# Grouping a unit's attention steps on TensorE, and pinning the convolution norm to VectorE's order, in a hybrid encoder layer on one core

## The chip, the cores and the metric

The kernel runs on one core of one Trainium2 chip. The core has five engines with queues of their own that run in order: TensorE (PE, with its weight loads shown as PEld), VectorE (DVE), ScalarE (ACT), GpSimd (POOL), and SyncE (SP), which issues most DMAs. The metric is device time in microseconds for one execution, as the median of the runs. Less is better.

## The reference

One encoder layer over 2048 tokens of width 1024, all in float32:

```
q, k, v, u = split(rmsnorm(x) @ w_in)              # 8 heads of 64; rotary on q and k
att  = dilated attention: windows (128,1), (512,4), (2048,16), merged by a softmax of their log-denominators
conv = silu(layernorm(depthwise_conv31(a * sigmoid(g)) + b))        # 512 channels
h = x + concat(att, conv) @ w_out
h = h + cross attention(rmsnorm(h), rmsnorm(mem))    # 4 heads of 256, 256 memory rows
h = h + square(relu(rmsnorm(h) @ w_up)) @ w_down     # 4096 hidden
out = rmsnorm(h)
```

For each window and dilation a query block of 128 rows sees a band of keys: `s = q k^T / 8`, a mask, `p = exp(s - max)`, `o = p v / sum(p)`. The layernorm of the convolution needs the mean and the variance over 512 channels for every token.

## The kernel before

Matrix products are split into high and low parts (`mm3`, L198 to L202): three products of 128x512 columns for each 128x128 weight tile, so `L200`, `L201` and `L202` on TensorE are all the large products. Weights come by DMA into `raw`; ScalarE rounds them (`whi`, L190) and VectorE takes the rest (`wlo`, L191).

The work has stages. First the memory's products and the input projections: `lin` for q, k and the gated convolution input, and `v` (values), whose results ScalarE and VectorE evict into `vst` (L575, L576). Beside the last of these VectorE computes the convolution of the first 512 tokens: one multiply-add of 128x512 for each of 31 taps (`cacc`, L217). Then comes the far stage: attention of the first 512 tokens, in which the windows of dilation 16 are computed for all tokens, interleaved with the remaining gated input products. Then four post blocks of 512 tokens each: `o` (output projection), `xs` and `x` (cross attention), and eight times `up` and `dn` (the MLP). Beside post block p run, as sides, the near attention of the next 512 tokens (`att(p+1)`) and their convolution (`conv`). These three stretches are the passes. The last post block has no side.

An attention unit is one half of one head's work for one pattern: two query blocks. It has three steps, as a generator with two `yield`s between them:

1. the scores on TensorE (`s`, L1003, four products of 256 columns), then on VectorE the mask and the minimum (`att_probs`, L774), and on ScalarE the exponential (L775) into `sm`;
2. `att_turn`: four transposes of `sm` on TensorE (`pt`, L781), and the split of the result into half-precision `ph` (ScalarE, L784) and `pl` (VectorE, L785);
3. `att_pv`: twelve half-precision products of the probabilities with the values (`opt`, L789 to L791), and their eviction.

Far units (`att_far`, L857 and L858) do the same for four blocks. The loop `att` keeps three units in flight: u at step 1, a at step 2, b at step 3.

The convolution's norm, `conv_ln`, has its own steps: it loads the four channel blocks (`lc`), adds them (`lsum`, L240 to L242), sums columns on TensorE (`lps`), broadcasts the mean (`lrb`), squares, sums again, takes a reciprocal root with GpSimd's power (L177), broadcasts it (`lrc`, L185), and ends in Silu on ScalarE (L268), a split and two stores.

The order on each engine is not the order of the program alone. A planner in the framework places instructions by its own estimate of when they are ready. `weave` sets how often a side is advanced per step of the main work, and `after(stack, "pe")` ties what is issued under it on TensorE behind the last recorded TensorE instruction (`last["pe"]`); `"dve"` does the same on VectorE. `pinned(gen, names)` applies that to every step of a generator. Unpinned steps may be placed earlier on an engine than the work that the program issued before them. On SP the loads of keys and queries (`load_keys`) stand among those of the weights; GpSimd makes the second ordering of the queries (`turned`, L822).

The change touches `conv` (L705), the loop of `att` (L1079 to L1086) and the line that makes `ln0`, the norm of the first 512 tokens (L1138).

Of the kernel before, what the change touches and what calls it, by code (L numbers as in the profile page):

```python
# [43 lines left out]
def f(ap):  # L44
    return ap.bitcast(F32)


def hybrid_layer(ctx, tc, A, out):
# [3 lines left out]
    def pool(name, space=None, stack=ctx, side="left"):  # L52
        kw = {"reuse_waits": "tile", "side": side} if space is None else {"space": space}
        return stack.enter_context(tc.tile_pool(name=name, bufs=1, **kw))

    def dma(o, i, q=None):
        (q or nc.sync).dma_start(o, i)
# [10 lines left out]
    def ps(kind, name, shape=(P, 512), dtype=F32):  # L68

        if isinstance(banks[kind], str):  # L70
            kind = banks[kind]
        n = turn.get(kind, 0)
        turn[kind] = n + 1
        return psp.tile(list(shape), dtype, tag=f"bank{banks[kind][n % len(banks[kind])]}", name=name)
# [3 lines left out]
    def after(stack, *names):  # L78
        for nm in names:
            if nm in last:  # L80
                stack.enter_context(tc.issue_after(last[nm].ins))

    def pinned(gen, *names):

        while True:
            with ExitStack() as st:
                after(st, *names)
                if next(gen, st) is st:
                    return
            yield  # L90
# [11 lines left out]
    def drain(*gens):  # L102
        for g in gens:
            for _ in g:
                pass
# [57 lines left out]
    def gain(key, k):  # L163
        if key == "mem":
            return gm[:, k:k + 1]
        c = GV[key] + k
        return gv[:, c:c + 1]
# [8 lines left out]
    def newton_rsqrt(dst, v, t):  # L176
        POOL.tensor_tensor(dst, v, mhalf.to_broadcast([P, v.shape[1]]), op=ALU.pow)  # L177
        DVE.tensor_tensor(t, dst, dst, op=ALU.mult)
        DVE.scalar_tensor_tensor(t, t, -0.5, v, op0=ALU.mult, op1=ALU.mult)
        DVE.scalar_tensor_tensor(dst, t, 1.5, dst, op0=ALU.add, op1=ALU.mult)  # L180

    def bcast_rows(dst_ps, col, n):

        for j in range(n):
            PE.transpose(dst_ps[:, j * P:(j + 1) * P], col[:, j:j + 1].to_broadcast([P, P]), ident)  # L185
# [37 lines left out]
    def conv_ln(n, alloc):  # L223
        sl = slice(512 * n, 512 * (n + 1))
        cs = []
        for c in range(4):
            t = alloc(f"cs{c}", F32, f"lc{n}_{c}")
            dma(t, cscr[c][:, sl])
            cs.append(t)
        sm = alloc("sum", F32, f"lsum{n}")  # L230
        q = alloc("q", F32, f"lq{n}")
        col = [alloc(f"col{i}", F32, f"lcol{n}{i}", (P, 4)) for i in range(3)]

        def colsum(key):
            pc = ps("c", f"lps{n}{key}")
            for j in range(4):
                last["pe"] = PE.matmul(pc[:, j:j + 1], sm[:, j * P:(j + 1) * P], ones[:, 0:1], start=True, stop=True)
            return pc[:, 0:4]

        DVE.tensor_tensor(sm, cs[0], cs[1], op=ALU.add)  # L240
        DVE.tensor_tensor(sm, sm, cs[2], op=ALU.add)
        DVE.tensor_tensor(sm, sm, cs[3], op=ALU.add)  # L242
        yield
        yield
        DVE.tensor_scalar(col[0], colsum("m"), -1.0 / DCONV, None, op0=ALU.mult)
        yield
        rb = ps("c", f"lrb{n}")
        bcast_rows(rb, col[0], 4)
        for c in range(4):
            DVE.tensor_tensor(cs[c], cs[c], rb, op=ALU.add)  # L250
        ACT.activation(sm, cs[0], AF.Square)
        for c in range(1, 4):
            ACT.activation(q, cs[c], AF.Square)
            DVE.tensor_tensor(sm, sm, q, op=ALU.add)
        yield
        yield
        yield
        DVE.tensor_scalar(col[1], colsum("v"), 1.0 / DCONV, EPS, op0=ALU.mult, op1=ALU.add)
        yield
        newton_rsqrt(col[0], col[1], col[2])  # L260
        yield
        rb2 = ps("c", f"lrc{n}")
        bcast_rows(rb2, col[0], 4)
        for c in range(4):
            DVE.tensor_tensor(cs[c], cs[c], rb2, op=ALU.mult)
        yield
        for c in range(4):
            ACT.activation(cs[c], cs[c], AF.Silu, bias=gain("ln_b", c), scale=gain("ln_g", c))  # L268
        for c in range(4):
            th_ = alloc("hi", F32R, f"lh{n}_{c}")  # L270
            tl_ = alloc("lo", F32R, f"ll{n}_{c}")
            ACT.copy(th_, cs[c])
            POOL.tensor_tensor(tl_, cs[c], f(th_), op=ALU.subtract)
            dma(f(cath[4 + c][:, sl]), f(th_))
            dma(f(catl[4 + c][:, sl]), f(tl_))
            yield
# [404 lines left out]
    def ln_tiles(pl):  # L681
        def alloc(role, dtype, name, shape=(P, 512)):
            if role[:3] == "col":
                return pl.tile(list(shape), F32, tag="cl_" + role, name=name)
            if role[:2] == "cs":
                return pl.tile(list(shape), F32, tag="u" if role[2] < "2" else "acc", name=name, bufs=2)
            return pl.tile(list(shape), dtype, tag="vr", name=name, bufs=2)
        return alloc

    def conv_units(pl, n, cs=(0, 1, 2, 3), ahead=True):  # L690
        def alloc(role, shape, name):
            return pl.tile(list(shape), F32, tag=role, name=name, bufs=2)

        u = conv_load(cs[0], n, alloc)
        yield
        yield
        for i, c in enumerate(cs):
            nxt = conv_load(cs[i + 1], n, alloc) if ahead and i + 1 < len(cs) else None
            yield from conv_unit(c, n, alloc, u)
            u = nxt or (conv_load(cs[i + 1], n, alloc) if i + 1 < len(cs) else None)  # L700

    def conv(pl, n):

        yield from pinned(conv_units(pl, n), "dve")
        yield from conv_ln(n, ln_tiles(pl))  # L705

    def both(*gens):
        for _ in zip(*gens):
# [84 lines left out]
    def low_parts(pl, n, bufs, tag):  # L793

        t = [pl.tile([P, n], F32R, tag=f"{tag}{i}", name=f"{tag}{i}") for i in range(bufs)]
        for x in t:
            POOL.memset(f(x[64:P]), 0.0)
        return t
# [268 lines left out]
    def att(p, far=None):  # L1067


        comb = iter(())  # L1070

        def then(pr, o0):
            nonlocal comb
            drain(comb)
            comb = combine(p, pr, o0)
            next(comb)

        a = b = None
        for u in chain(att_units(p, far, then), (None, None)):  # L1079
            if u:  # L1080
                next(u)
            yield
            if a:
                next(a)
            if b:
                next(b, None)  # L1086
            next(comb, None)
            yield
            a, b = u, a
        for _ in comb:  # L1090
            yield
# [13 lines left out]
    def ahead(m):  # L1105
        raw = wp.tile([P, 8, P], F32, tag="raw", name=f"raw_o0{m}", bufs=2)
        dma(raw, wcols(w_out, m * P))
        yield
        wout[m] = wsplit2(wp, raw, f"o0{m}")
        turn_w[0] += 1  # L1110
        yield
# [3 lines left out]
    with ExitStack() as st:  # L1115
        p2_ = pool("att_far", stack=st, side="right")
        p2_.tile([P, 16, 144], F32R, tag="k3", name="k3", bufs=2)
        qlow3 = low_parts(p2_, 1024, 2, "ql3")
        p2_.tile([P, 176], F32, name="farpad")
        rest = pinned(pipeline(*(u for c in range(4) for u in glu(c, (2, 3), True)), ahead(0), ahead(1)), "pe")  # L1120
        for _ in range(38):
            next(rest)

        c01 = []

        def ln_alloc(role, dtype, name, shape=(P, 512)):

            if role[:3] == "col":
                return top.tile(list(shape), F32, tag="cl_" + role, name=name)
            if role in ("cs0", "cs1"):  # L1130
                if not c01:
                    c01.append(aq.tile([P, 2, 512], F32, tag="ld", name="lc01"))
                return c01[0][:, int(role[2])]
            if role in ("cs2", "cs3", "sum"):
                return aq.tile(list(shape), F32, tag={"cs2": "cth", "cs3": "ctl", "sum": "cat"}[role], name=name)
            return t2(name, dtype)

        ln0 = pinned(conv_ln(0, ln_alloc), "pe")  # L1138
        first = pinned(att(0, p2_), "pe")
        weave(islice(first, 50), (ln0, 0.33), (rest, 0.75))  # L1140
        drain(ln0)
        weave(islice(first, 74), (rest, 0.75))
        drain(rest)
# [458 lines left out]
```

## Time and profile before

| | us |
|---|---|
| median of 3 runs | 2862.2 |
| lowest and highest | 2858.24, 2862.79 |
| the profiled execution | 2865.75 |
| its span, first to last instruction | 2864.0 |

The profile is of one execution. On its page, groups of instructions stand by line, engine, operation and tiles, with their count, busy time and mean duration. TensorE's matrix products are pipelined: the next starts before the last one's shown end, so the time from start to start is what a product costs. A bracket at the end of a timeline row gives the idle time of the engine before that row, and what ended it. The windows view gives, for a stretch, the busy time of each engine and the clock that TensorE was granted (1.00 is full).

### The profile page before, as it was taken

The numbers are of one execution on the slowest core, as the hardware profiler recorded it, in microseconds if no ns is written. First come the engines' busy times: TensorE is split into PE (matmuls) and PEld (weight loads), VectorE is DVE, ScalarE is ACT, GpSimd is POOL, SyncE is SP. The second block draws the span as 40 slices with busy tenths as digits, with TensorE's granted clock in tenths as the row PEclk, the third lists the DMA queues.
The fourth block names the chain that finished last, engine by engine and source line by source line (L and its number), as shares of the span: only waits on it lengthen the run. The fifth ranks groups of instructions, "written<-read, shape, count | busy, mean of one in ns | idle before, by whom it ended". The sixth has DMA issues, their size and how long they took to land.

```text
span 2864.0 us, 41201 instructions
## 1 busy us (share of the span) xinstructions
PE 2807.4 (98%) x15440; PEld 2359.9 (82%) x15440; DVE 1960.8 (68%) x3473; ACT 1206.4 (42%) x2055; POOL 467.7 (16%) x483
## 2 busy tenths in 40 slices
PE   8999999999999999999999999999999999999998
PEld 7878899888788888888888888888888888888887
DVE  5736535455789777566887865579886646569886
ACT  5633211365544333434543344344433434444443
POOL 1337431131202011200021112001120110000000
PEclk9999999999999999999999999999999999999999
DMA  8979854699734544545444535534544455223332
GB/s 251 302 174 230 197 146 126 170 244 241 221 108 128 143 127 130 160 146 175 120 132 126 148 113 165 177 122 123 143 121 136 141 158 177 89 82 102 90 117 67
DMA packets 590730, 434.27 MB, mean 152 GB/s; under 512 B 191582, under 2 KB 508434, under 8 KB 590017
## 3 DMA queue, kind: packets, MB, share of 16 engines
q1 hardware_dynamic: 549776, 407.68, 50.5%
q10 hardware_dynamic: 38528, 17.93, 2.5%
q0 software_dynamic: 2224, 6.01, 0.6%
q8 instruction: 122, 2.00, 0.3%
q14 instruction: 80, 0.65, 0.1%
HBM read 340.42 MB, written 91.11 MB: 151 GB/s over the span
## 4 chain that ended last, share of the span: by engine, by line
PE 83%; DVE 8%; DMA 5%; issue 1%; ACT 1%; POOL 1%; SPq 1%; DVEq 0%; POOLq 0%; ACTq 0%
PE dn L200 8%; PE dn L201 8%; PE dn L202 8%; PE up L200 7%; PE up L202 7%; PE up L201 7%; PE lin L200 4%; PE lin L202 4%; PE lin L201 4%; PE o L200 2%; PE o L202 2%; PE o L201 2%; DVE cacc L217 2%; PE xs L200 2%; PE xs L202 2%; PE xs L201 2%
## 5 line engine op out<-in xcount | busy, mean ns | idle before, releaser
L200 PE MATMUL up<-mh,whi_u 128*128 128x512 f32 x1024 | 403.5, 394 | 0.4 <-ACT mh L1219 0.4
L201 PE MATMUL up<-ml,whi_u 128*128 128x512 f32 x1024 | 399.6, 390 | 2.1 <-DVE ml L1220 2.1
L202 PE MATMUL up<-mh,wlo_u 128*128 128x512 f32 x1024 | 399.1, 390 | 0.0
L217 DVE SCALAR_TENSOR_TENSOR cacc<-cu,cw,cacc 128x512 f32<-128x512 f32 x480 | 386.1, 804 | 5.4
L200 PE MATMUL dn<-hhh,whi_d 128*128 128x512 f32 x768 | 299.1, 399 | 1.1 <-ACT hhh L1331 1.1
L201 PE MATMUL dn<-hhl,whi_d 128*128 128x512 f32 x768 | 298.7, 391 | 0.7 <-DVE hhl L1332 0.7
L202 PE MATMUL dn<-hhh,wlo_d 128*128 128x512 f32 x768 | 298.2, 391 | 0.0
L190 ACT CAST whi_u<-raw_u 128x1024 fp32r<-128x1024 f32 x128 | 134.5, 1051 | 263.2 <-PE dn L201 188.7
L190 ACT CAST whi_d<-raw_d 128x1024 fp32r<-128x1024 f32 x100 | 105.1, 1051 | 319.9 <-PE up L201 281.5
L201 PEld LDWEIGHTS up<-ml,whi_u 128*128 128x128 f32 x1024 | 192.5, 188 | 40.9 <-DVE ml L1220 3.4
L202 PEld LDWEIGHTS up<-mh,wlo_u 128*128 128x128 f32 x1024 | 192.3, 188 | 40.4
L200 PEld LDWEIGHTS up<-mh,whi_u 128*128 128x128 f32 x1024 | 192.4, 188 | 38.0 <-ACT mh L1219 0.6
L191 DVE TENSOR_TENSOR wlo_u<-raw_u,whi_u 128x1024 fp32r<-128x1024 f32 x128 | 161.3, 1261 | 43.4 <-ACT whi_u L190 43.1
L1345 DVE TENSOR_TENSOR h<-h,dn 128x512 f32<-128x512 f32 x192 | 128.6, 683 | 84.7 <-PE dn L202 83.9
L1329 DVE SCALAR_TENSOR_TENSOR rl<-up,ssumx 128x512 f32<-128x512 f32 x96 | 66.0, 690 | 171.0 <-PE up L202 170.3
L774 DVE CUSTOM_DVE_ANT_0 sm<-s,mask 128x256 f32<-128x256 f32 (+1 forms) x384 | 128.6, 375 | 69.0 <-PE s L1003 45.2
L202 PEld LDWEIGHTS dn<-hhh,wlo_d 128*128 128x128 f32 x768 | 144.2, 188 | 30.7
L200 PEld LDWEIGHTS dn<-hhh,whi_d 128*128 128x128 f32 x768 | 143.7, 188 | 29.7 <-ACT hhh L1331 1.3
L201 PEld LDWEIGHTS dn<-hhl,whi_d 128*128 128x128 f32 x768 | 144.6, 188 | 28.3 <-DVE hhl L1332 1.5
L177 POOL TENSOR_TENSOR nr<-st_v,mhalf 128x4 f32<-128x4 f32 (+1 forms) x15 | 14.3, 951 | 817.2 <-DVE st_v L173 817.2
L775 ACT ACTIVATE sm<-sm,o 128x256 f32<-128x256 f32 (+1 forms) x288 | 116.5, 454 | 55.7 <-DVE o L774 55.3
L191 DVE TENSOR_TENSOR wlo_d<-raw_d,whi_d 128x1024 fp32r<-128x1024 f32 x100 | 128.2, 1282 | 14.2 <-ACT whi_d L190 14.1
(459 smaller groups left out, 7075.3 us busy)
## 6 DMA issues: line engine op xcount, KB each, us to landing
raw_u<-in_w_up_dram SPq DMA_DIRECT2D x128, 512.0 KB
raw_d<-in_w_down_dram SPq DMA_DIRECT2D x100, 512.0 KB
raw_o<-in_w_out_dram SPq DMA_DIRECT2D x32, 512.0 KB
raw_a<-ascr SPq DMA_DIRECT2D x32, 512.0 KB
raw_b<-bscr SPq DMA_DIRECT2D x32, 512.0 KB
b<-in_w_down_dram SPq DMA_DIRECT2D x28, 512.0 KB
k<-kscr SPq DMA_DIRECT2D x24, 512.0 KB
k<-kscr SPq DMA_DIRECT2D x8, 1152.0 KB
```

Source lines behind the costliest of these rows:

```text
L177: POOL.tensor_tensor(dst, v, mhalf.to_broadcast([P, v.shape[1]]), op=ALU.pow)
L190: ACT.copy(hi, raw)
L191: (lo_eng or DVE).tensor_tensor(lo, raw, f(hi), op=ALU.subtract)
L200: PE.matmul(o, lh, rh, start=first, stop=False, skip_group_check=more)
L201: PE.matmul(o, lh, rl, start=False, stop=False, skip_group_check=more)
L202: last["pe"] = PE.matmul(o, ll, rh, start=False, stop=end, skip_group_check=more)
L217: DVE.scalar_tensor_tensor(acc, u[:, t:t + 512], cw[:, c, t:t + 1], acc, op0=ALU.mult, op1=ALU.add)
L774: last["dve"] = DVE.tensor_tensor_reduce(dst, so, mask[:, 256 * m:256 * m + nk], 1.0, 3e38, ALU.add, ALU.min, mn)
L775: last["act"] = ACT.activation(dst, dst, AF.Exp, bias=mn, scale=-1.0)
L1329: last["dve"] = DVE.scalar_tensor_tensor(r, pt, 0.0, rsb, op0=ALU.max, op1=ALU.mult)
L1345: last["dve"] = DVE.tensor_tensor(hs[m], hs[m], pt, op=ALU.add)
```

## The change

In the passes the scores of unit u move from the beginning of the loop's turn to its end, after the transposes of unit a and the products of unit b, and the products and the scores are each tied behind the last recorded TensorE instruction. The far stage keeps the order that it had. The norm of the passes is pinned to VectorE's order, and the first norm, pinned to TensorE's before, to both.

```diff
     def conv(pl, n):
 
         yield from pinned(conv_units(pl, n), "dve")
-        yield from conv_ln(n, ln_tiles(pl))
+        yield from pinned(conv_ln(n, ln_tiles(pl)), "dve")
...
         for u in chain(att_units(p, far, then), (None, None)):
-            if u:
+            if u and far:
                 next(u)
             yield
-            if a:
-                next(a)
-            if b:
-                next(b, None)
+            for g in (a, b, None if far else u):
+                with ExitStack() as st:
+                    if not far and g is not a:
+                        after(st, "pe")
+                    if g:
+                        next(g, None)
             next(comb, None)
             yield
             a, b = u, a
...
-        ln0 = pinned(conv_ln(0, ln_alloc), "pe")
+        ln0 = pinned(conv_ln(0, ln_alloc), "pe", "dve")
```

## The prediction

> **What bounds the kernel now.** I read the page first, then the busy time by stage, then TensorE's own waits.
>
> ```profile
> span 2864.0 us, 41201 instructions
> PE 2807.4 (98%) x15440; PEld 2359.9 (82%) x15440; DVE 1960.8 (68%) x3473; ACT 1206.4 (42%) x2055; POOL 467.7 (16%) x483
> PE 83%; DVE 8%; DMA 5%; issue 1%; ACT 1%; POOL 1%; SPq 1%; DVEq 0%; POOLq 0%; ACTq 0%
> ```
>
> TensorE is busy for 98% of the span and carries 83% of the chain, so only what makes TensorE stand still or issue slower counts. Next, the windows: the far stage (541 to 770 us) and the three passes in which the near attention runs beside the post block (770 to 2262). The columns are length, TensorE busy, weight load, VectorE, ScalarE, GpSimd, granted clock, DMA.
>
> ```profile
> 541.00:770.00 229.00, 213.47 (x1847) 186.85 (x1847) 139.91 (x548) 137.12 (x326) 57.35 (x77) 0.96 0.87 229
> 770.00:1290.00 520.00, 518.09 (x2743) 428.27 (x2742) 391.86 (x653) 221.65 (x355) 74.00 (x75) 1.00 0.48 137
> 1290.00:1836.00 546.00, 543.70 (x2886) 450.26 (x2885) 397.15 (x670) 227.07 (x364) 76.13 (x76) 1.00 0.48 140
> 1836.00:2262.00 426.00, 423.78 (x2324) 351.05 (x2323) 327.96 (x566) 177.14 (x295) 55.06 (x56) 1.00 0.47 135
> ```
>
> The passes, where the grouping acts, hold 1492.00 - 1485.57 = 6.4 us of idle TensorE, at full clock: little can be won there by removing waits. The larger waits are earlier. From TensorE's list of waits over the span, and two of the same list for the passes alone:
>
> ```profile
> PE opt L791 <- DVE pl L785: 6.9, 9, 1.4
> PE s L858 <- DMA ql<-qfar: 4.3, 2, 2.2
> PE lin L200 <- DVE vst L576: 4.1, 1, 4.1
> ```
>
> ```profile
> PE up L201 <- DVE ml L1220: 2.1, 3, 0.9
> PE catT L948 <- POOL cat L940: 1.5, 2, 1.2
> ```
>
> The third row is one single wait. The timelines of VectorE and TensorE around it, and the windows behind it, say what it is:
>
> ```profile
> 506.08 0.69 DVE L240 TENSOR_TENSOR lsum<-lc 128x512 f32<-128x512 f32 x1 [9.44 <-DMA lc<-cscr]
> 521.58 0.69 DVE L242 TENSOR_TENSOR lsum<-lsum,lc 128x512 f32<-128x512 f32 x1 [5.97 <-DMA lc<-cscr]
> ```
>
> ```profile
> 513.56 0.80 PE L200 MATMUL lin<-xh,whi_g 128*128 128x512 f32 x1 [4.09 <-DVE vst L576]
> ```
>
> ```profile
> 513.50:518.30 4.80, 4.74 (x11) 3.78 (x12) 2.08 (x5) 0.00 (x0) 0.00 (x0) 0.50 0.35 111
> 518.30:524.00 5.70, 5.70 (x26) 4.70 (x26) 0.69 (x1) 0.60 (x1) 1.45 (x2) 1.00 0.99 255
> ```
>
> A sum of the convolution norm (L240) stands in VectorE's queue among the evictions of the value products and waits 9.44 us for a load. The evictions behind it (L576) come late, the banks stay full, and TensorE stops for 4.09 us. Then the clock is at half for 4.80 us.
>
> **The change part by part.**
>
> *The first norm (L1138, now pinned to VectorE too).* In the changed kernel's built order the three sums L240 to L242 no longer stand among the value evictions. They follow the score steps of the second far unit. The wait of 4.09 us goes. The half clock goes with it: 11 products took 4.80 us where the next window's 5.70 / 26 = 0.22 us each would give 2.4, so 2.4 are lost. Term 1 is -(4.1 + 2.4) = **-6.5**; its bounds are -6.5 and 0, zero if another wait of that length takes its place. Nothing of the norm is late next: the sums stand behind the last load's landing in these rows (521.58 us). The sums, 3 x 0.69 = 2.1 us, now lie in the far stage, where VectorE is busy 139.91 of 229.00 us; I cost them at nothing. If that cover fails, products there (`opt`, 6.9 us of waits already) wait up to 2.1 longer. The norm's later steps also move there by a few places, on ScalarE (Silu) and on SP, where half of one head's far queries are issued after two output stores; this end is bounded by the 2.2 us that such a load has cost once. I take 0 for both.
>
> *The norms of the passes (L705).* The same pin. No norm wait shows on TensorE's list for the passes, so it is worth 0; its limit is the 6.4 us of all waits there.
>
> *The grouping (L1079 to L1086).* No instruction is added or removed on TensorE (15,356 matrix instructions in both built orders). Three things change: the order inside a step, where the scores stand, and how long after them their transposes come.
>
> The first is a price for each time the stream goes from the half-precision products (`opt`) back to 32-bit work. A piece of the timeline in the first pass:
>
> ```profile
> 919.00 0.36 PE L1003 MATMUL s<-k,qt 128*128 128x256 f32 x1
> 919.20 0.29 PE L1003 MATMUL s<-k,ql 128*128 128x256 f32 x1
> 919.32 0.28 PE L1003 MATMUL s<-k,qt 128*128 128x256 f32 x1
> ...
> 920.55 0.48 PE L200 MATMUL up<-mh,whi_u 128*128 128x512 f32 x1
> 920.86 0.40 PE L201 MATMUL up<-ml,whi_u 128*128 128x512 f32 x1
> ```
>
> Starts tell the cost, since busy spans overlap. The scores at 919.00 follow `opt` products and hold the next start for 0.20 us, where the following one holds it 0.12; the `up` product at 920.55 follows `opt` and holds it 0.31 against the 0.22 above. So 0.08 to 0.09 us per change. Counted in the two built orders, `opt` is followed by something else 261 times before and 229 after (by matrix products 175 and 90, by scores 23 and 91, by transposes 37 and 41, by others 26 and 7). Term 2 is -32 x 0.08 = **-2.6**. Its bounds are -3 and 0.
>
> The second: scores were issued up to one step ahead of their unit's turn, and the planner could hoist them further. Now they stand behind the older unit's products. The buffers of keys and queries come free later, so SP issues those loads (two `qh`, one `ql`, one `k` per head) behind weight loads that they preceded, and GpSimd turns the queries (L822) later. Each is needed some three units on, about 30 us of TensorE work by the pitch above, so I cost it at 0; the limit is again 2.2 us per load that comes late.
>
> The third is the risk. By counting products between a unit's scores and its transposes, the median falls from about 18 us of TensorE work to about 9.5, and in 17 of 96 units to under 6.2. In that time VectorE must mask and take the minimum (L774) and ScalarE the exponential (L775). The quickest and one of the slowest in the first pass:
>
> ```profile
> 806.43 0.30 PE L1003 MATMUL s<-k,ql 128*128 128x256 f32 x1
> ```
>
> ```profile
> 806.76 0.42 DVE L774 CUSTOM_DVE_ANT_0 sm<-s,mask 128x256 f32<-128x256 f32 x1 [1.27 <-PE s L1003]
> ```
>
> ```profile
> 807.23 0.91 ACT L775 ACTIVATE sm<-sm,o 128x256 f32<-128x256 f32 x2
> ```
>
> ```profile
> 886.31 0.29 PE L1003 MATMUL s<-k,ql 128*128 128x256 f32 x1
> ```
>
> ```profile
> 892.82 0.90 ACT L775 ACTIVATE sm<-sm,low 128x256 f32<-128x256 f32 x2
> ```
>
> From the end of the scores to the end of the exponentials it takes 1.4 us where VectorE is free and 7.1 where it has a backlog. The tightest place is the start of the first pass's `up` stage, with some 2.2 us between the two. I walk it:
>
> ```profile
> 907.66 0.94 PE L1180 MATMUL nps<-ones,ssumx 128*128 128x1 f32 x8
> ```
>
> ```profile
> 911.25 0.16 DVE L173 TENSOR_SCALAR st_v<-nps 128x4 f32<-128x4 f32 x1
> ...
> 914.36 1.22 DVE L191 TENSOR_TENSOR wlo_d<-raw_d,whi_d 128x1024 fp32r<-128x1024 f32 x1
> 915.50 0.74 DVE L217 SCALAR_TENSOR_TENSOR cacc<-cu,cw,cacc 128x512 f32<-128x512 f32 x1
> 916.16 0.68 DVE L785 TENSOR_TENSOR pl<-pt,ph 128x512 f16<-128x512 f32 x1
> ```
>
> After the norm's column sums (`nps`) the new order has 31 `up` products (31 x 0.22 = 6.8 us), one attention group and four broadcasts (1.8) before the transposes: 8.6 us. VectorE has `st_v`, two weight splits (914.36 to 915.50, 1.14 each), four taps (0.66 each), one `pl` (0.6), two mask steps (0.7) and small steps (0.6), 6.8 in all, then ScalarE 0.9 and 0.1 for the hand-over: 7.8. If VectorE starts when `nps` ends there is no wait. If it is as late as in the rows (911.25 against 908.60, 2.65 us), the transposes wait 10.4 - 8.6 = 1.8. Eight more `up` products now precede `nps` (1.8 us), which eats most of that lateness, so I am nearer to 0 here. Over the 17 tight units I take four waits of about 1 us (the size of the 0.9 above), less 2 us of the present 6.4, which fall at the same `up` and `dn` starts. Term 3 is **+2**. Its bounds are -6.4 and +17 (each tight unit 1 us late).
>
> The sum is -6.5 - 2.6 + 2 = -7.1. The profiled execution took 2865.75 us (its span and 1.75 around it), 3.55 above the median of the runs, so 2858.65 for such an execution and 2862.2 - 7.1 = **2855.1** for the median.
>
> **The clock, row and rule.** What does a wait cost beyond itself?
>
> ```profile
> 736.68 0.20 PE L791 MATMUL opt<-v,pl 128*128 128x65 f16 x1 [1.39 <-DVE pl L785]
> ```
>
> ```profile
> 737.00:740.20 3.20, 3.20 (x14) 2.62 (x12) 0.22 (x1) 0.38 (x1) 1.43 (x2) 0.50 0.98 259
> 1760.00:1768.00 8.00, 6.82 (x33) 5.40 (x32) 5.76 (x6) 3.48 (x5) 3.25 (x2) 1.00 0.43 123
> ```
>
> A wait of 1.39 us was followed by 3.2 us at half clock, 1.6 us lost; the `catT` wait of 1.2 us, inside the second window, was not. So a new wait of 1.4 us or more is priced at itself plus 1.6. The Trainium skill (TensorE: Matmul & The Clock Gate, section "HAM oscillation — how this bites in real kernels") sets the rule at no idle gap above about 3.4 us, watched in a free-running window (Part 1). By that rule waits of this size are free of the clock, and the slower rival below would come to 2864.5 instead of 2869.3 (three times 1.6 less), no longer slower; the row at 736.68 disagrees with it, and I go by the row.
>
> **The rivals.**
> - *Slower: the transposes wait for VectorE.* Place: the `up` and `dn` starts of each pass. Price per pass: 1.8 + 1.6 for the clock at the walked place and 1.0 at two more, 5.4, or 16.2 in three passes; 2862.2 - 9.1 + 16.2 = 2869.3. It decides from 14.8 us in the passes, 4.9 per pass. For it: VectorE had backlogs of 7.1 us; against: the planner puts transposes where it holds them ready, and on TensorE's list for the passes stands no wait for an exponential.
> - *The stall moves.* The first norm's waits or the far queries' loads return the 6.5 us in the far stage: 2862.2 - 2.6 + 2 = 2861.6. For it: 15.5 us of idle there (229.00 - 213.47); against: the sums find VectorE free.
> - *Better: the present waits of the passes go too.* 2862.2 - 9.1 - 6.4 = 2846.7. Against: the two rows above show the post block's and the combine's waits, which the change doesn't touch.
> - *The grouping does not happen.* In the built order 48 of 96 groups stand whole, the others have matrix products inside. If the change of precision then costs what it did, 2862.2 - 6.5 = 2855.7.
>
> **How the numbers follow.** Forecast 0.52, slower 0.17, stall moves 0.15, better 0.10, no grouping 0.06. The bound between faster and same is 0.2%, 5.7 us, about what runs of this kernel can tell from no change. The forecast's own range is 2850 to 2859, so some 0.44 of its 0.52 is faster; with "better" and half of "no grouping" 0.57. Slower is most of its rival, 0.15. The rest, 0.28, is same. The range runs from 2847 to 2870, the two outer rivals.
>
> **What would show it.** Right: no `lin <- vst` wait and no half clock near 515 us; L240 after the first far scores; `opt` changes about 0.08 us each. Wrong: `pt <- sm` or `opt <- pl` rows with over 5 us per pass, half clock inside the passes, or far-stage idle above 20 us.

## The result, and the profile after

The change is slower: 2875.91 us (median; 2871.87 to 2882.25), against 2858.14 for the kernel before in the same comparison. The ratio is 1.0062, with a 95% interval of 1.0046 to 1.0077, or some 18 us. The forecast was 2855.1, below the kernel before; the time also lies outside its range. The profiled execution took 2882.25 us, the slowest of them, with a span of 2880.3. The lines of the changed kernel's page that answer to those shown of before (lines of the code behind the loop of `att`, which ended at L1086, have moved down by two):

```profile
span 2880.3 us, 41197 instructions
PE 2807.7 (97%) x15440; PEld 2362.3 (82%) x15440; DVE 1962.6 (68%) x3473; ACT 1213.0 (42%) x2055; POOL 463.7 (16%) x483
```

TensorE's busy time hardly moved (2807.4 before). The span grew by 16.3 us, so TensorE stands still longer. Its waits in the passes, as the list of waits has them (us in total, times, longest):

```profile
PE catT L948 <- POOL cat L940: 5.6, 2, 4.0
PE x L200 <- ACT xp L1261: 4.2, 3, 1.4
PE ptx L1272 <- DVE ptl L1275: 2.9, 3, 1.0
PE xs L200 <- ACT xp L1261: 2.4, 3, 0.8
PE x L200 <- ACT pth L1274: 2.0, 3, 0.7
PE up L200 <- DVE rl L1331: 1.9, 2, 0.9
PE pt L781 <- ACT ssumx L1312: 1.8, 1, 1.8
PE nrb L185 <- DVE nr L180: 1.4, 2, 0.7
PE dn L200 <- DVE h L1347: 0.4, 2, 0.2
```

These add up to 22.6 us, where the passes had 6.4. Rows 2 to 5 come three times each, once per pass, and all belong to the cross-attention's softmax: row 4 stands halfway through its scores (`xs`), where the banks come round again, row 2 at the hand-over from the scores to the output (`x`), rows 3 and 5 some 10 us into `x`. The first row is the combination of the attention parts. The walked place, `pt` at the start of `up`, waited once, for 1.8.

The windows of the changed kernel add the clock (columns as in the prediction: length, TensorE, weight load, VectorE, ScalarE, GpSimd, granted clock, DMA):

```profile
918.40:921.80 3.40, 3.40 (x20) 2.92 (x17) 3.40 (x6) 3.37 (x8) 0.00 (x0) 0.50 0.13 39
1218.70:1222.10 3.40, 3.40 (x11) 2.82 (x12) 2.30 (x3) 1.29 (x3) 0.00 (x0) 0.51 0.69 194
1409.90:1413.30 3.40, 3.40 (x23) 2.93 (x23) 1.10 (x2) 0.96 (x2) 0.00 (x0) 0.50 0.00 0
2027.70:2031.10 3.40, 3.40 (x10) 2.62 (x9) 3.40 (x5) 3.40 (x9) 1.68 (x4) 0.50 0.00 0
```

Four stretches at half clock, 1.7 us lost in each, 6.8 together; in the passes of before no window of 10 us was below 0.99. So the passes lost 16.2 us in waits (22.6 - 6.4) and 6.8 in clock in this execution.

What the change was to win by the first norm is there. The stretch of the old wait runs at full clock without idle time:

```profile
506.00:520.00 14.00, 14.00 (x79) 12.25 (x78) 0.85 (x2) 1.34 (x3) 1.84 (x2) 1.00 0.78 186
```

Up to the first `o` product the changed profile is 9.3 us ahead (it starts at 727.9 us, against 737.2). Not all of that is the first norm's: in the profiles of two kernels below that keep the old first norm (the hold on the norms of the passes alone, and the group alone) `o` starts at 729.7 and 729.4 us. From its first `o` to the first `o` of the last post block the change takes 26.3 us longer: TensorE's idle time in that stretch grows from 8.3 to 28.8 us, and it holds five stretches at half clock instead of one. The last post block is 0.7 shorter.

### The profile page after: what moved, and what is told of

The parts are those of the page before. It is cut to its first block, busy times and chain, and to the rows that moved or that the text cites. A ratio compares the mean times of both kernels' runs of the same rounds, so it can differ in the third digit from the quotient of the medians.

```text
span 2880.3 us, 41197 instructions
## 1 busy us (share of the span) xinstructions
PE 2807.7 (97%) x15440; PEld 2362.3 (82%) x15440; DVE 1962.6 (68%) x3473; ACT 1213.0 (42%) x2055; POOL 463.7 (16%) x483
## 5 line engine op out<-in xcount | busy, mean ns | idle before, releaser
L217 DVE SCALAR_TENSOR_TENSOR cacc<-cu,cw,cacc 128x512 f32<-128x512 f32 x480 | 392.5, 818 | 5.2
L822 POOL CAST qt<-qh 128x512 fp32r<-128x512 f32 x24 | 35.6, 1482 | 808.2 <-PE s L1003 802.6
```

The lines of the kernel that those rows point to most:

```text
L217: DVE.scalar_tensor_tensor(acc, u[:, t:t + 512], cw[:, c, t:t + 1], acc, op0=ALU.mult, op1=ALU.add)
L822: POOL.tensor_copy(d.rearrange("p (b i) -> p b i", b=4), t.rearrange("p (i b) -> p b i", b=4))
```

## The experiments

The theory formed from these two profiles: the group, not the norms, makes the loss, and makes it in the cross-attention, around the hand-over from `xs` to `x`, where each bank's softmax (a minimum and a scale on VectorE, an exponential on ScalarE) must end before the bank is used again. The rivals: the norm's hold does it; the group loses at many tight places; the group costs on its own and the norms give little back.

**The parts alone.** The first norm's hold alone:

```diff
-        ln0 = pinned(conv_ln(0, ln_alloc), "pe")
+        ln0 = pinned(conv_ln(0, ln_alloc), "pe", "dve")
```

> Only the first norm is pinned to VectorE's order; the grouping and the passes are as before. If the value stage's stall is the whole worth of this pin (theory A and theory B alike), TensorE's wait of 4.1 us for vst and the half clock after it are gone and the time is 6 to 9 us below before. If the stall only moves into the far stage, the time is within 2 us of before and the far stage's idle TensorE grows from 15.5 us to about 22.

Measured: 2851.88 us, ratio 0.9982 [0.9973, 0.9991], 5 us below the kernel before. The gain is real, somewhat under the expected size.

The hold on the norms of the passes alone:

```diff
-        yield from conv_ln(n, ln_tiles(pl))
+        yield from pinned(conv_ln(n, ln_tiles(pl)), "dve")
```

> Only the norms of the passes are pinned to VectorE's order. Theory A (the loss is the grouping's, in the cross attention): within 3 us of before. Theory B (the held-back norm delays the combine and the post block, as the longer waits for cat in the changed kernel suggest): 6 us or more above before, with waits of catT for cat of about 4 us.

Measured: 2858.20 us, 1.0008 [0.9998, 1.0018], no difference that can be told from none.

The group alone, the change with both norms put back:

```diff
-        yield from pinned(conv_ln(n, ln_tiles(pl)), "dve")
+        yield from conv_ln(n, ln_tiles(pl))
...
-        ln0 = pinned(conv_ln(0, ln_alloc), "pe", "dve")
+        ln0 = pinned(conv_ln(0, ln_alloc), "pe")
```

> Only the grouping; both norms as before. Theory A: 24 to 28 us above before, since the whole loss is here and the first norm's gain is missing. Theory B: 10 us above before or less. In both, the wait of 4.1 us for vst is back.

Measured: 2870.42 us, 1.0047 [1.0032, 1.0062], 13 us above. The group is the main cost. Both expectations missed the size. The wait for `vst` is back, as expected, but at 2.2 us.

**Where the group loses.** The change, but with the old order from the end of the output projection to the end of the cross-attention:

```diff
+    cross = [False]
...
-            if u and far:
+            early = far or cross[0]
+            if u and early:
                 next(u)
...
-            for g in (a, b, None if far else u):
+            for g in (a, b, None if early else u):
                 with ExitStack() as st:
-                    if not far and g is not a:
+                    if not early and g is not a:
...
         pr_, late = {}, []
+        cross[0] = True
...
         yield from xl
+        cross[0] = False
```

> The changed kernel, but between the end of the output projection and the start of the MLP each unit's scores stand first and nothing is tied, as before; so the grouping acts beside the output projection and the MLP alone. Theory A: the waits for xp, ptx and pth (about 4.9 us in each of three passes) are gone, and the time is 13 to 17 us below the changed kernel, 1 to 5 us above before. Theory B: within 4 us of the changed kernel.

Measured: 2858.38 us, 0.9997 [0.9987, 1.0006]; 0.65% below the change's ratio, some 18 us, and back at the kernel before. Most of the loss sits in the cross-attention, but not all: this kernel has both holds on the norms, and the same two without any group measure 0.9978 (below), so some 5 us stay. In its profile `catT` still waits for `cat`, 4.9 us in two places. The windows over `xs` and `x` of the three passes say how much; the sum of the three lengths, and TensorE's busy time in them, first of the kernel before:

```profile
1338.90:1445.00 106.10, 105.86 (x605) 87.82 (x604) 88.87 (x175) 51.66 (x100) 7.64 (x6) 1.00 0.38 111
...
sum 317.00, PE 316.32 PEld 262.73 DVE 269.01 ACT 155.46 POOL 21.47; mean PE 105.44 PEld 87.58 DVE 89.67 ACT 51.82 POOL 7.16
```

and of the change:

```profile
1342.50:1454.40 111.90, 107.97 (x605) 89.01 (x604) 85.52 (x167) 52.10 (x99) 10.57 (x8) 0.98 0.39 110
...
sum 331.40, PE 319.77 PEld 264.69 DVE 260.87 ACT 156.57 POOL 31.80; mean PE 106.59 PEld 88.23 DVE 86.96 ACT 52.19 POOL 10.60
```

605 matrix instructions in both, VectorE busy less and not more, and 14.4 us longer. How that comes shows on three engines at the same spot, the second pass's start of `x`. Before (VectorE, ScalarE, TensorE):

```profile
1386.80 0.68 DVE L1256 TENSOR_REDUCE xmx<-xs 128x2 f32<-128x512 f32 x1
...
1388.05 0.22 DVE L1257 TENSOR_SCALAR xmx<-xmx,nr 128x2 f32<-128x2 f32 x1
```

```profile
1388.37 0.56 ACT L1259 ACTIVATE xp<-xs,xmx,nr 128x256 f32<-128x256 f32 x1 [0.95 <-DVE xmx L1257]
```

```profile
1390.62 0.39 PE L202 MATMUL xs<-whi_a,yl 128*128 128x512 f32 x1
...
1391.60 0.48 PE L200 MATMUL x<-pth,whi_b 128*128 128x512 f32 x1
```

After, the same engines in the same order:

```profile
1390.49 0.42 DVE L774 CUSTOM_DVE_ANT_0 sm<-s,mask 128x256 f32<-128x256 f32 x1
...
1392.44 1.28 DVE L1258 TENSOR_REDUCE xmx<-xs 128x2 f32<-128x512 f32 x2
1393.64 0.74 DVE L217 SCALAR_TENSOR_TENSOR cacc<-cu,cw,cacc 128x512 f32<-128x512 f32 x1
1394.30 0.68 DVE L1258 TENSOR_REDUCE xmx<-xs 128x2 f32<-128x512 f32 x1
1394.90 0.35 DVE L1259 TENSOR_SCALAR xmx<-xmx,nr 128x2 f32<-128x2 f32 x2
```

```profile
1396.15 0.57 ACT L1261 ACTIVATE xp<-xs,xmx,nr 128x256 f32<-128x256 f32 x1
```

```profile
1394.24 0.39 PE L202 MATMUL xs<-whi_a,yl 128*128 128x512 f32 x1
...
1397.41 0.50 PE L200 MATMUL x<-pth,whi_b 128*128 128x512 f32 x1 [1.41 <-ACT xp L1261]
```

Before, the first exponential starts 2.3 us before the last `xs` product. After, VectorE does the group's masks and a tap, then three minima with a tap among them, and only then scales the first: the first exponential starts 1.9 us after the last `xs` product, and `x` waits 1.41 for a bank.

**Is it VectorE's order?** The change, with each bank's minimum held behind the scale step of the bank before it, and later taps behind that scale:

```diff
-            DVE.tensor_reduce(mx, sp_.rearrange("p (z m) -> p z m", z=2), axis=AX.X, op=ALU.min)
-            DVE.tensor_scalar(mx, mx, rs[:, t:t + 1], None, op0=ALU.mult)
+            with ExitStack() as st:
+                if t:
+                    after(st, "soft")
+                DVE.tensor_reduce(mx, sp_.rearrange("p (z m) -> p z m", z=2), axis=AX.X, op=ALU.min)
+            last["soft"] = last["dve"] = DVE.tensor_scalar(mx, mx, rs[:, t:t + 1], None, op0=ALU.mult)
```

> The change with one more order on VectorE: in the cross-attention each bank's minimum stands behind the scale step of the bank before it, and later taps stand behind that scale step. Theory A (the cross-attention's first products wait because VectorE takes three minima, mask steps and taps before it scales the first): the 1.4 us waits for the exponential at the start of the x products go in all three passes, the x stages come out 1 to 2 us shorter each than in the change, the time 3 to 6 us below the change's. Theory B (TensorE's own order finishes the first bank late, VectorE's order follows from it): the waits stay within 0.5 us, the time within 2 us of the change's.

Measured: 2862.87 us, 1.0018 [1.0007, 1.0029], 0.44% below the change's ratio, some 12.6 us; more than expected. The waits of `x` for `xp` are gone. The `xs` stages are shorter and not the `x` stages, as theory A had it: work that stood in one now stands in the other, and only their sum tells. In this kernel:

```profile
1380.46 0.23 DVE L1262 TENSOR_SCALAR xmx<-xmx,nr 128x2 f32<-128x2 f32 x1
```

```profile
sum 321.00, PE 315.68 PEld 263.74 DVE 269.12 ACT 159.97 POOL 31.22; mean PE 105.23 PEld 87.91 DVE 89.70 ACT 53.32 POOL 10.41
```

The scale step stands 3.6 us before the first `x` product (1384.08 us), and 10.4 of the 14.4 us are back. That order could be a gain for any kernel, so the control has it on the first norm alone, without the group (that diff and the first norm's, nothing else):

> The control for the softmax steps in turn: the same order on VectorE, on the first norm alone, without the group. Theory A (taking the softmax steps in turn gives back what the group took, and there is nothing to give back here, since the minima and scale steps alternate already): within 3 us of the first norm alone, 2849 to 2855 us, with xs stages within 0.5 us of the kernel before. Theory B (taking them in turn shortens the cross-attention whatever stands before it, so the 13 us that it took off the change do not tell of the group): 4 to 12 us below the first norm alone, xs stages 1 us or more shorter.

Measured: 2853.55 us, 0.9979 [0.9970, 0.9988], the same as without it (0.9982), as theory A had it; the sum of its windows is 317.11. Taking the steps in turn is worth nothing by itself. It gives back what the group took.

**The hold on the norms of the passes, beside the group.** The change without it:

```diff
-        yield from pinned(conv_ln(n, ln_tiles(pl)), "dve")
+        yield from conv_ln(n, ln_tiles(pl))
```

> The change without the hold on the norms of the passes; TensorE's order is that of the change, instruction for instruction. Theory A (the norm's hold costs nothing by itself and 7 to 10 us beside the group, since GpSimd's step of the combination then stands behind the norm's split, which waits for ScalarE): 8 us above the kernel before, the 4 us wait of catT for cat in the second pass's MLP gone. Theory B (the difference between the change and its parts is scatter of the runs): 13 us above or more, as the group alone less the first norm's 5 would give 8, and the norm's hold adds 0 and not 10.

Measured: 2869.31 us, 1.0041 [1.0028, 1.0055], between the expectations; its interval overlaps those of the change and of the group alone. `catT` no longer waits for `cat`. The same pair with the softmax steps in turn, by the diff above, where the runs scatter less:

> The change with the softmax steps in turn, less the hold on the norms of the passes. Theory A (the pass norms' hold costs 4 to 7 us beside the group): 2856 to 2859 us, the wait of catT for cat (5.6 us in two places with the hold) under 2 us. Theory B (the hold costs nothing beside the group either): within 2.5 us of 2862.9.

Measured: 2859.54 us, 1.0002 [0.9993, 1.0012], against 1.0018 with the hold: 4.6 us by the ratios, the size of theory A, though the two intervals overlap. With the hold, the list of waits for the passes has the row below; without it, it has no `catT` row.

```profile
PE catT L948 <- POOL cat L940: 5.6, 2, 3.3
```

GpSimd's timeline in the change shows the way, and TensorE's the end of it:

```profile
1208.81 1.30 POOL L273 TENSOR_TENSOR ll<-lc,lh 128x512 fp32r<-128x512 f32 x1 [4.99 <-ACT lh L272]
1210.07 1.22 POOL L933 TENSOR_TENSOR ce<-ce,csm 128x24 f32<-128x24 f32 x1
```

```profile
1218.62 1.04 PE L948 MATMUL catT<-ident,cat 128*128 128x128 f32 x4 [3.98 <-POOL cat L940]
```

GpSimd stands 4.99 us before a split of the norm that waits for ScalarE, and the combination's steps stand behind that split. That the hold is what makes ScalarE late there is read from the order, and was not tested apart. Is that the hold's price in any company? The kernel before with both holds, and no group:

```diff
-        yield from conv_ln(n, ln_tiles(pl))
+        yield from pinned(conv_ln(n, ln_tiles(pl)), "dve")
...
-        ln0 = pinned(conv_ln(0, ln_alloc), "pe")
+        ln0 = pinned(conv_ln(0, ln_alloc), "pe", "dve")
```

> Both holds on the norms, the first and those of the passes, without the group. Theory A (the hold on the passes' norms costs only beside the group, where the combination's steps come late on GpSimd): as the first norm alone, ratio 0.998, and no wait of catT for cat over 2 us. Theory B (it costs 4 to 6 us in any company, and the run of it alone, 1.0008 with an interval up to 1.0018, hid it): at the kernel before, ratio 0.9995 to 1.0005.

Measured: 2852.55 us, 0.9978 [0.9969, 0.9987], as the first norm alone, and the longest wait of `catT` for `cat` is 1.1 us. So the hold costs only beside the group. That fits the 5 us that stayed when the group was kept out of the cross-attention, since there the hold still stood beside the group.

**What the group is worth elsewhere.** The group in the MLP alone, with the first norm's hold and the passes' norms as before; the flag of above now covers a post block from its start:

```diff
+    cross = [True]
...
     def post(p):
+        cross[0] = True
...
         yield from xl
+        cross[0] = False
```

> The first norm pinned to VectorE as in the change, the norms of the passes as before, and the group kept to the time from the end of the block's cross-attention to the end of its MLP; from a block's start to the end of the cross-attention products the old order of scores, transposes and products stands. Theory A (the group loses in the output projection and the cross-attention and gains 0.7 to 2.3 us in each of three MLP stages): 3 to 5 us below the first norm alone, so 8 to 10 us below the kernel before (ratio 0.9965 to 0.9972). Theory B (the MLP gains of the changed profiles are scatter, and the group is worth nothing there either): at the first norm's own 5 us below (ratio 0.998). Above 0.999: the group costs in the MLP too, and the profiles' stage lengths were misread.

Measured: 2850.58 us, 0.9975 [0.9965, 0.9985]; and with the softmax steps in turn as well:

> The first norm, the group in the MLP alone, and the softmax steps in turn. Theory A: as the group in the MLP alone, 2848 to 2854 us. Theory B: 4 to 12 us below that, so under 2847 us and the fastest kernel here.

Measured: 2850.93 us, 0.9977 [0.9968, 0.9986]. Neither can be told from the first norm alone (0.9982). So theory A of the first of these two is not borne out, though its interval does not exclude it; theory A of the second is. The MLP stages that looked shorter (in the profile of the group alone, by 2.3, 0.8 and 0.7 us) are partly work moved out of them. The windows of the second pass for the scores (L1003) alone, MLP and then the `o` stage, in the kernel before:

```profile
1445.00:1835.70 390.70, 16.96 (x94) 14.36 (x92) 1.00 0.48 138
1289.70:1338.90 49.20, 0.00 (x0) 0.00 (x0) 1.00 0.69 216
```

and in the change:

```profile
1454.40:1845.30 390.90, 15.00 (x80) 11.01 (x80) 1.00 0.48 136
1291.80:1342.50 50.70, 2.41 (x12) 1.71 (x12) 1.00 0.71 217
```

Twelve scores went from the MLP into `o`, whose 1.5 us more are these (249 matrix instructions in that stage before, 261 after).

**The order without the ties.** The group's order in the program, without the two ties, norms as before:

```diff
-                with ExitStack() as st:
-                    if not far and g is not a:
-                        after(st, "pe")
-                    if g:
-                        next(g, None)
+                if g:
+                    next(g, None)
```

> The group's order in the program (transposes, products, next scores) without the ties to TensorE's last step of the group, norms as before; TensorE changes 276 times away from a run of the half-precision products, against 261 before and 226 in the group alone. Theory A (the ties make the group, and the group's late softmax steps at the cross-attention make the loss): within 4 us of the kernel before, the waits at the first cross-attention products gone. Theory B (the loss comes from the scores being issued last in the program, with or without ties): 8 us above or more, with the same waits at the first cross-attention products.

Measured: 2862.75 us, 1.0020 [1.0010, 1.0031], between the two. The hand-over's waits are gone, as theory A had it, but another wait came in the MLP, `dn` for the low half of the hidden rows, 5.0 us in six places. Why the planner's order puts it there was not followed further.

The fastest kernels are five of the six that hold the first norm and do not group in the cross-attention, 2850.6 to 2853.6 us; the sixth (2858.38 us) has the hold on the norms of the passes beside the group. All five are faster than the kernel before and the change; among themselves they cannot be told apart.

## Why the prediction was wrong

- **Term 1 (first norm, -6.5): right in mechanism, its size that of one execution.** The wait and the half clock are gone, and the sums run from 538.9 us, not among the value evictions. Alone it measured -5.1. But the three profiles that keep the old first norm and its place among the evictions (the pass norms' hold alone, the group alone, the order without the ties) show the same wait at 1.7, 2.2 and 2.1 us, and behind the first of them no half clock. Beside the group the gain cannot be told from none (1.0041 with it, 1.0047 without).
- **The norms of the passes at 0: right alone, wrong in company.** Without the group 1.0008 and 0.9978 (with the first norm); beside the group 4.6 us. The step priced the pin by VectorE's order and TensorE's list of waits, and did not follow the norm's split onto GpSimd's queue, which the combination shares.
- **Term 2 (changes of precision, -2.6): the price and the count hold, the name does not.** From start to start, the median `up`, `dn`, `xs`, `o` or `x` product takes 314 ns behind an `opt` product and 227 behind another such product, in both kernels, so 0.09 us per change as priced, and `opt` is followed by something else 261 and 229 times in the two profiles, as counted. But 32-bit transposes are as dear a neighbour (314 to 316 ns), so the price does not need a change of precision. Products and scores that follow `opt`, transposes or other short products fell from 262 to 228 between the first `o` and the first `o` of the last post block, 3.0 us at 87 ns. TensorE's busy time there, less the half clock, is only 1.1 us shorter (1640.1 - 8.5 against 1634.3 - 1.6); what took the rest was not followed. The group in the MLP alone shows no gain that can be measured, and there the number of such changes did not fall (264).
- **Moves on SP and GpSimd at 0: not contradicted.** No wait for a load of keys or queries stands on the list for the passes.
- **Term 3 (+2): the step that failed.** It held 17 units with little time between scores and transposes to be the risk, and counted waits of those transposes. They waited once, for 1.8 us, at the walked place, which the walk had as its upper end. That the two agree is in part luck: VectorE started 2.85 us after `nps` ended, so the lateness that the prediction took to be mostly eaten was all there; the exponentials ended 10.5 us after `nps` (the walk's late case has 10.4), which accounts for 1.2 us of the wait, and the rest is ScalarE's copy L1312 behind them, the releaser that the profile names, which the walk did not have. The loss came from other work on VectorE: the cross-attention's softmax, whose order against the group's masks and the taps the group also moved. Four places per pass wait there now, for 0.8, 1.4, 1.0 and 0.7 us, 11.5 in the three passes. With the softmax steps put in turn on VectorE 12.6 us of the run time came back. In the profiled execution the passes lost 16.2 in waits and 6.8 in clock, where the term had +2.
- **The rival "slower"** had the direction, 2869.3 us, and the amount that decides (14.8 us in the passes), but the wrong place and instruction. Its mark, `pt` waiting for `sm` with over 5 us per pass, did not appear; the half clock inside the passes did. The idle time of the far stage grew from 15.5 to 18.8 us (219.70 - 200.88 from 541 to 760.7 us, the changed kernel being 9.3 ahead), short of the 20 that the prediction named; 2.5 of the growth are `opt` waiting for `pl` (9.4 against 6.9).
- **The clock.** That a short wait can bring half clock was right, and the price too (1.7 us a time, priced at 1.6). That every new wait of 1.4 us or more brings it was not: of six such waits in the passes two were followed by half clock, and two more stretches followed shorter waits; see the last section.

What remains open: against the control (first norm and softmax steps in turn, 0.9979) the change loses some 24 us by the ratios. 12.6 came back with the softmax steps in turn and 4.6 with the hold on the pass norms left out; with both, the group still costs some 6.6 us (1.0002 against 0.9979). 321.00 - 317.11 = 3.9 of it stand in the `xs` and `x` windows, by the profiles with the hold and of the control. TensorE's waits show more of it: between the first `o` and the first `o` of the last post block it is idle for 13.9 us in the one kernel and 7.0 in the control, and the largest wait that it has and the control has not stands in the MLP, once per pass:

```profile
PE dn L200 <- DVE h L1350: 5.4, 3, 1.8
```

Which of the moved steps makes `h` late there was not tested.

## What to carry to other kernels

When a change reorders one engine that is busy all the time, list every short chain that crosses engines and must hand a buffer back to it, also of work that the diff does not touch, and look up in the built orders of all engines where its steps now stand. Here that list would have held the softmax between `xs` and `x` and the combination's steps on GpSimd; the prediction looked only at the instructions that moved. And when stage lengths are compared, count the instructions in each stage first, since a planner that moves work across a stage's edge makes a gain on one side and a loss on the other.

## What the hardware showed beside that

Short waits can be followed by half clock. Of the four stretches above, one followed the `catT` wait of 3.98 us and one the `pt` wait, and two followed still shorter ones:

```profile
917.67 0.66 PE L781 MATMUL pt<-ident,sm 128*128 128x128 f32 x4 [1.82 <-ACT ssumx L1312]
...
1409.64 1.45 PE L200 MATMUL x<-pth,whi_b 128*128 128x512 f32 x3 [0.67 <-ACT pth L1274]
...
2027.13 0.50 PE L200 MATMUL up<-mh,whi_u 128*128 128x512 f32 x1 [0.94 <-DVE rl L1331]
```

The last two each had another wait just ahead of them (0.96 us at 1407.71, 0.70 us at 2025.08). The Trainium skill (TensorE: Matmul & The Clock Gate, section "HAM oscillation — how this bites in real kernels") states the rule as no idle gap of TensorE above some 3.4 us; three of the four stretches came after shorter gaps, so the traces here do not agree with it as a bound. A short wait does not always bring it: the kernel with the softmax steps in turn had waits up to 3.3 us in its passes and no window of 10 us there under 0.99. The wait of `dn` for `h`, 1.8 us long, shows it best: it comes three times in that kernel and three times in the same kernel without the pass norms' hold; none of the first three is followed by half clock, and two of the other three are. So the length of one wait does not decide it, and what does is not shown here.

The second finding is that a large product costs 87 to 89 ns more not only behind half-precision products, but as much behind 32-bit transposes. In the kernel before, the product at 847.32 holds the next start for 0.23 us, and the one behind two transposes for 0.32:

```profile
847.32 0.40 PE L201 MATMUL x<-ptl,whi_b 128*128 128x512 f32 x1
847.55 0.38 PE L1270 MATMUL ptx<-ident,xp 128*128 128x128 f32 x2
847.69 0.48 PE L202 MATMUL x<-pth,wlo_b 128*128 128x512 f32 x1
848.01 0.38 PE L1270 MATMUL ptx<-ident,xp 128*128 128x128 f32 x2
```

The scores, of 256 columns, cost nothing extra behind a large product (117 to 120 ns, against 122 to 123 behind another score), and a large product behind scores takes 232 to 233 ns. All the dear neighbours have 128 columns or fewer; whether that is the reason was not tested.
